# Output-projection weights of a hybrid diffusion layer: the gate's half row kept on chip while w_out is scaled, and its two parts in one raw tile

## The chip, the cores and the metric

The kernel runs on one core of one Trainium2 chip. The metric is the device time of one execution in microseconds (us). An execution with a profile also has a span, from its first to its last instruction on the engines, which is a little shorter than its time.

Five engines run side by side: PE (TensorE, matmuls, with PEld for its weight loads), DVE (VectorE), ACT (ScalarE), POOL (GpSimd) and SP (SyncE, which here issues nearly all transfers, in order). Each takes its instructions in order. Instructions of different engines wait for each other through semaphores.

## What is computed

One layer of a backbone for 2048 latent tokens of width 1024 behind a context of 256 tokens. Cut to what matters here:

```python
sh1, sc1, g1, sh2, sc2, g2 = split(ada, 6)        # ada = silu(c) @ w_ada + b_ada, rows of 1024
h = modulate(rmsnorm(x, norm_mix), sh1, sc1)
p = h @ w_in                                      # 1024 -> 3584 columns
o = concat(hgrn2_both_directions(p), spatial_gating(p))   # 4 heads of 128 each
x = x + g1 * (o @ w_out)                          # w_out is 1024 x 1024
h2 = modulate(rmsnorm(x, norm_ffn), sh2, sc2)
a, g = split(h2 @ w_up, 2)                        # 2 x 2816 columns
x = x + g2 * ((a * gelu(conv3x3(g))) @ w_down)    # w_down is 2816 x 1024
return rmsnorm(x, norm_final)
```

All inputs and the output are float32. The gates `g1` and `g2` scale columns, so `g1 * (o @ w_out)` equals `o @ (w_out * g1)`: the kernel scales the columns of the two weight matrices once, ahead of their use.

## The kernel before, in words

The large products run as three matmuls on values split in two parts: a high part, which is the value rounded to the format that PE multiplies fast (called fp32r in the profile), and a low part, the difference. `split` makes them with a cast on ACT (L133) and a difference on DVE or POOL (L134); `mm3` and `run_banks` do high x high, high x low, low x high.

**Phase one** (to about 975 us) makes `o` from `x`. It goes over the 2048 tokens in two halves of 1024. For each half and each of the four heads of the scan (`hg`), and for the four heads of the positional gating (`sgu`), it takes 128 columns of `w_in` at a time, splits them and multiplies: `run_banks` steps through a list of banks, each of 512 tokens by 128 columns in PSUM and 24 matmuls. Two banks in a row share a column block. The raw columns come into a tile `raw` (`raw_tile`, 128 x 1024 float32, a ring of three), are fetched at L221, cast to `whi` (L133) and subtracted to `wlo` (L134), one column block ahead of PE.

Between groups of three matmuls `run_banks` calls `slot()`, which lets two queues of smaller work step forward, `hg_q` and `bg_q`. Each piece of such work is a generator. When it says `yield w`, it takes its next step at the first slot after another `w` us of PE time have been issued, by the kernel's own count (`Tensor.t`). The scan's levels lie in `hg_q`: L514 (queries), L591 to L594 (keys), L794 to L801 (the diagonal), L846 (into the scores). In `bg_q` lie, from the first head on and one after the other: eight blocks of adaLN rows (`ada_block`), which leave `g1` and `g2` as rows in DRAM (`g_d`, stored at L971), then `w_out_ops`, `conv_taps` and `w_down_ops`. What `bg_q` still holds near the end of phase one is run down at once by `open_wo`.

So a generator fixes the order in which the program asks for its instructions. The build tool then puts the instructions of every engine in order by its own estimate of durations, with the program's order as priority and buffers handed out as they come free. It may take a load ahead of where the program asks for it; instructions passed through `pin` keep the program's order.

**`w_out_ops`** (L982 to L997) scales `w_out` and splits it, in 16 tiles of 128 rows by 512 columns: row blocks `k` outside, column halves `n` inside. One raw tile holds the weights in its left half and the gate's half row, spread over all 128 partitions, in its right half; both are fetched for each tile (L989, L990). After 5 us of PE time DVE multiplies (L993), ACT casts the high part into the tile `wo_hi` (tag `acc`, one buffer, which `ada_block` and `w_down_ops` use too), DVE writes the low part over the gate, and SP stores the two parts to `wo_d` (L995, L996). Another 2.5 us later the next tile begins. At the end of phase one and the beginning of the next, `wo_d` is fetched again as weights of the output projection (L916, L1145).

**`w_down_ops`** (L999 to L1011) scales `w_down` by `g2` in 22 tiles of 256 rows by 512 columns. It fetches the gate's half row once for each column half, into `acc` (L1004), then the weights (L1007), multiplies 9 us of PE time later (L1009, pinned), and stores (L1010).

**Phase two** is the output projection, the gated MLP by a scheme with seven products instead of eight, and the last norm. The change doesn't touch it.

Of the kernel before, what the change touches and what calls it, by code (L numbers as in the profile page):

```python
# [9 lines left out]
F32 = mybir.dt.float32  # L10
F32R = mybir.dt.float32r
# [7 lines left out]
P = 128  # L19
D = 1024  # L20
NK = D // P
# [27 lines left out]
def view(t, off, dims):  # L49

    return bass.AP(t.tensor, t.offset + off, [list(t.ap[0])] + [list(d) for d in dims])
# [32 lines left out]
def tile_trunk(ctx, tc, x, c, cx, c_ctx, w_ada, b_ada, norm_mix, norm_ffn, w_in, hg_norm, sgu_g, sgu_b,  # L84
               w_sp, b_sp, w_out, w_up, conv_w, conv_b, w_down, norm_final, masks, out):
    nc = tc.nc
    V, S, G, T = nc.vector, nc.scalar, nc.gpsimd, Tensor(nc.tensor)
    ld = nc.sync.dma_start
    st = nc.sync.dma_start
# [25 lines left out]
    g_d = dr.tile([2, D], F32, name="g_d")  # L115
# [3 lines left out]
    wo_d = dr.tile([P, NK, 2, D], F32, name="wo_d")  # L119
# [11 lines left out]
    def split(hi, lo, raw, eng=None, keep=lambda i: i):  # L131

        keep(S.copy(hi, raw))  # L133
        (eng or G).tensor_sub(lo, raw, hi.bitcast(F32))  # L134
# [56 lines left out]
    with es1:  # L191
        ps = es1.enter_context(tc.tile_pool(name="ps1", bufs=1, space=PSUM, reuse_waits="tile"))
        p1 = es1.enter_context(tc.tile_pool(name="p1", bufs=1, reuse_waits="tile"))
        pm = es1.enter_context(tc.tile_pool(name="pm", bufs=1, reuse_waits="tile"))
# [19 lines left out]
        def raw_tile():  # L214
            return p1.tile([P, D], F32, tag="raw", name="raw", bufs=3)
# [52 lines left out]
        acc = ph.tile([P, 2, 512], F32, tag="qs", name="acc")  # L268
# [712 lines left out]

        def w_out_ops():  # L982

            for k in range(NK):
                for n in range(2):
                    cl = slice(n * 512, n * 512 + 512)
                    raw = raw_tile()
                    w, g = raw[:, :512], raw[:, 512:]
                    ld(w, w_out[k * P:(k + 1) * P, cl])  # L989
                    ld(g, g_d[0:1, cl].broadcast_to([P, 512]))  # L990
                    yield 5.0
                    hi = pm.tile([P, 512], F32, tag="acc", name="wo_hi")
                    V.tensor_mul(w, w, g)  # L993
                    split(hi.bitcast(F32R), g.bitcast(F32R), w, V)
                    st(wo_d[:, k, 0, cl], hi)  # L995
                    st(wo_d[:, k, 1, cl], g)  # L996
                    yield 2.5  # L997

        def w_down_ops():  # L999

            for n in range(2):
                cl = slice(n * 512, n * 512 + 512)
                g = pm.tile([P, 512], F32, tag="acc", name="g2")
                ld(g, g_d[1:2, cl].broadcast_to([P, 512]))  # L1004
                for j in range(NF // 2):
                    raw = raw_tile().rearrange("p (a c) -> p a c", a=2)
                    ld(raw, w_down[2 * j * P:2 * (j + 1) * P, cl].rearrange("(a p) c -> p a c", p=P))  # L1007
                    yield 9.0
                    pin(V.tensor_mul(raw, raw, view(g, 0, [[0, 2], [1, 512]])))  # L1009
                    st(wd_d[j][:, :, cl], raw)  # L1010
                    yield 2.5  # L1011

        def silu(dst, scale):
            def f(n0, n, pj):
# [5 lines left out]
        def head(hh, h):  # L1020
# [18 lines left out]
            def pre_g():  # L1039
                if prev[0] >= 0:  # L1040
                    need(hg_q, (prev[0], prev[1], "keys"))
                else:
                    need(bg_q, "x1")
                    for e in range(8):
                        bg_q.add(ada_block(e))
                    bg_q.add(w_out_ops())
                    bg_q.add(conv_taps())
                    bg_q.add(w_down_ops())
                t["F"] = pk.tile([P, 2, TH], F32, tag="F", name="F", align_bytes=AL)
                t["K"] = pk.tile([P, 2, TH], F32, tag="K", name="K", bufs=2, align_bytes=AL)  # L1050
# [135 lines left out]
    def zbank():  # L1186
        return ps2.tile([P, 512], F32, tag="uz", name="uz", bufs=2)
# [379 lines left out]
    for n, (u, i) in enumerate(prods):  # L1567
# [10 lines left out]
        p = zbank() if i == 1 else u.z if i in (4, 6) else u.x  # L1578
        hi, lo = u.A[i]
# [40 lines left out]
    V = Kept(nc.vector, pin)  # L1620
# [243 lines left out]
```

## Time and profile before

| What | Value |
|---|---|
| median of 3 runs | 2441.4 us |
| lowest and highest of the 3 runs | 2441.0 and 2443.07 us |
| the profiled execution | 2443.78 us |
| its span | 2442.0 us |
| instructions | 32331 |
| moved by DMA in the span | 400.10 MB |
| first to last product of `w_out_ops` (L993) | 366.9 to 498.2 us |
| first to last product of `w_down_ops` (L1009) | 542.3 to 829.8 us |

How to read the rows: times are us from the span's start, unless marked ns. A group's row gives line, engine, operation and tiles (`out<-in`), then how often it ran and the durations in ns (least, median, greatest) with its first and last start. A row of waits reads "who, at which line, `<-` for whom: us in total, times, longest". A row of the timeline begins with start and duration; in brackets stands how long the engine was idle just before, and what it waited for. A row of transfers gives the size of one and the median us from its issue to its landing. A busy PE isn't PE at its peak: matmuls are pipelined and their ends are modelled, so the record of one lasts longer than its share of PE's time.

### The profile page before, as it was taken

How to read it: one execution, taken by the hardware profiler on the slowest of the kernel's cores; microseconds unless marked ns; L12 is line 12 of the kernel's file. 1: busy time of each engine (PE TensorE's matmuls, PEld its weight loads, DVE VectorE, ACT ScalarE, POOL GpSimd, SP SyncE). 2: the span in 40 equal slices, each digit the busy share in tenths (PEclk: the TensorE clock that was granted, in tenths of full speed). 3: DMA queues.
4: the chain of work that ended last, by engine and by line, in shares of the span. 5: the costliest groups of instructions: out<-in, count | busy, mean ns of one | idle time of the engine just before them, and what ended most of it. 6: DMA issues, size and time to landing. Idle time of an engine off the chain costs nothing.

```text
span 2442.0 us, 32331 instructions
## 1 busy us (share of the span) xinstructions
PE 2403.1 (98%) x11711; PEld 1994.7 (82%) x11711; DVE 1659.9 (68%) x2253; ACT 1044.4 (43%) x1802; POOL 869.2 (36%) x788
## 2 busy tenths in 40 slices
PE   8999999999999999999999999999999999999998
PEld 5887888888888887787888888888888887888887
DVE  5757796666786785465596666639866672776875
ACT  4554344444344443354544443435445442332343
POOL 0021110110122122000688788887888870000002
PEclk9999999999999999999999999999999999999999
DMA  8365446563354324668922322563222238934745
GB/s 308 120 202 165 147 147 212 186 226 124 108 175 154 105 103 162 221 208 254 312 77 89 100 77 94 175 233 101 86 94 84 86 112 338 322 122 147 228 153 197
DMA packets 307853, 400.10 MB, mean 164 GB/s; under 512 B 33113, under 2 KB 216161, under 8 KB 304621
## 3 DMA queue, kind: packets, MB, share of 16 engines
q1 hardware_dynamic: 304404, 397.28, 48.2%
q8 instruction: 92, 1.51, 0.2%
q10 hardware_dynamic: 3289, 0.76, 0.1%
q14 instruction: 68, 0.56, 0.1%
HBM read 288.85 MB, written 109.13 MB: 163 GB/s over the span
## 4 chain that ended last, share of the span: by engine, by line
PE 48%; issue 2%; DVE 1%; POOL 1%; ACT 1%; DMA 1%; SPq 0%; POOLq 0%; ACTq 0%; DVEq 0%
PE ux L65 19%; PE dn L65 15%; PE uz L65 14%; POOL ra L1723 0%; POOL rr L1724 0%; DMA raw<-in_w_up_dram 0%; DMA yf<-yd 0%; DVE dn L1434 0%; POOL Al L134 0%; ACT mhl L133 0%; ACT jk L1715 0%; DVE odd L80 0%; DVE fl L134 0%; ACT odd L1793 0%; DVE cv L1358 0%
## 5 line engine op out<-in xcount | busy, mean ns | idle before, releaser
L1434 DVE SCALAR_TENSOR_TENSOR dn<-gp,taps,dn 128x1024 f32<-128x1024 f32 x352 | 448.2, 1285 | 97.7 <-ACT dn L1431 93.3
L65 PE MATMUL dn<-thl,mhl 128*128 128x512 f32 x1680 | 381.5, 389 | 1.2 <-ACT thl L133 1.2
L65 PEld LDWEIGHTS dn<-thl,mhl 128*128 128x128 f32 x1680 | 315.0, 188 | 67.7 <-ACT thl L133 2.1
L134 POOL TENSOR_TENSOR Al<-raw,Ah 128x512 fp32r<-128x512 f32 x264 | 343.2, 1316 | 69.1 <-ACT Ah L133 42.7
L65 PE MATMUL pj<-xh,whi 128*128 128x512 f32 x896 | 362.5, 405 | 0.3 <-ACT whi L133 0.3
L65 PE MATMUL pj<-xl,whi 128*128 128x512 f32 x896 | 351.5, 392 | 0.0
L65 PE MATMUL pj<-xh,wlo 128*128 128x512 f32 x896 | 350.8, 392 | 0.8 <-DVE wlo L134 0.8
L133 ACT CAST Ah<-raw 128x512 fp32r<-128x512 f32 x264 | 162.9, 620 | 237.5 <-PE ux L65 127.7
L65 PE MATMUL ux<-xah,Ah 128*128 128x512 f32 x528 | 205.7, 390 | 0.3 <-ACT keep L1498 0.3
L65 PEld LDWEIGHTS pj<-xh,wlo 128*128 128x128 f32 x896 | 168.3, 188 | 36.8 <-DVE wlo L134 1.2
L65 PEld LDWEIGHTS pj<-xh,whi 128*128 128x128 f32 x896 | 168.7, 188 | 34.3 <-issue 3.5
L65 PEld LDWEIGHTS pj<-xl,whi 128*128 128x128 f32 x896 | 168.9, 188 | 29.9 <-DVE xl L253 0.2
L65 PE MATMUL dn<-wo,o 128*128 128x512 f32 x768 | 184.5, 397 | 2.6 <-ACT o L133 1.1
L65 PE MATMUL uz<-yf,Ah 128*128 128x512 f32 x704 | 174.0, 389 | 0.0
L65 PEld LDWEIGHTS dn<-wo,o 128*128 128x128 f32 x768 | 143.1, 189 | 32.8 <-ACT o L133 1.5
L591 POOL TENSOR_TENSOR K<-K,tot 128x512 f32<-128x512 f32 x40 | 61.1, 1526 | 300.3 <-DVE tot L521 203.9
L65 PE MATMUL ux<-yf,Ah 128*128 128x512 f32 x528 | 155.4, 389 | 0.0
L65 PEld LDWEIGHTS uz<-yf,Ah 128*128 128x128 f32 x704 | 132.1, 188 | 27.4
L65 PE MATMUL ux<-xah,Al 128*128 128x512 f32 x528 | 141.8, 390 | 1.0 <-POOL Al L134 1.0
L65 PE MATMUL ux<-xal,Ah 128*128 128x512 f32 x352 | 137.1, 389 | 0.0
L1723 POOL TENSOR_SCALAR ra<-ss 128x1 f32<-128x1 f32 x8 | 5.3, 663 | 360.4 <-ACT jk L1715 360.4
L134 DVE TENSOR_TENSOR wlo<-raw,whi 128x1024 fp32r<-128x1024 f32 x68 | 84.6, 1244 | 70.9 <-ACT whi L133 69.4
(341 smaller groups left out, 4456.1 us busy)
## 6 DMA issues: line engine op xcount, KB each, us to landing
raw<-in_w_up_dram SPq DMA_DIRECT2D x88, 512.0 KB, 3.6
mr<-m SPq DMA_DIRECT2D x85, 512.0 KB, 5.2
raw<-in_w_in_dram SPq DMA_DIRECT2D x68, 512.0 KB, 4.3
sT<-wd SPq DMA_DIRECT2D x88, 256.0 KB, 4.0
raw<-in_w_ada_dram SPq DMA_DIRECT2D x32, 512.0 KB, 4.2
yf<-yd SPq DMA_DIRECT2D x14, 1024.0 KB
m<-cv SPq DMA_DIRECT2D x22, 544.0 KB
raw<-in_w_down_dram SPq DMA_DIRECT2D x22, 512.0 KB, 3.8
```

What stands on the lines that cost most here:

```text
L65: return self.engine.matmul(out, lhsT, rhs, **kw)
L133: keep(S.copy(hi, raw))
L134: (eng or G).tensor_sub(lo, raw, hi.bitcast(F32))
L591: e.tensor_mul(view(K2, row * W + o, src), view(K, o, src), view(tot, t0, [[4, n], [ts, 2], [0, B]]))
L1434: V.scalar_tensor_tensor(out=cr, in0=gt[:, t // 3:t // 3 + RH, t % 3:t % 3 + GW], scalar=taps[:, t * NF + f:t * NF + f + 1], in1=cr, op0=A ...
L1723: G.tensor_scalar(out=a, in0=ss, scalar1=plus, scalar2=None, op0=ALU.add)
```

## The change

In `w_out_ops` the column halves become the outer loop. The gate's half row is fetched once for each half, into a tile of the tag `acc`, and stays there for eight row blocks. A raw tile now has the weights in its second half and receives the high part in its first; the low part is written over the weights. One store takes both parts to `wo_d`. The product is asked for 8 instead of 5 us of PE time after the load, and the next tile 1.5 instead of 2.5 us after the store. In `w_down_ops` the two waits go from 9 and 2.5 us to 8 and 2.

```diff
         def w_out_ops():
 
-            for k in range(NK):
-                for n in range(2):
-                    cl = slice(n * 512, n * 512 + 512)
-                    raw = raw_tile()
-                    w, g = raw[:, :512], raw[:, 512:]
+            for n in range(2):
+                cl = slice(n * 512, n * 512 + 512)
+                g = pm.tile([P, 512], F32, tag="acc", name="g1")
+                ld(g, g_d[0:1, cl].broadcast_to([P, 512]))
+                for k in range(NK):
+                    raw = raw_tile().rearrange("p (a c) -> p a c", a=2)
+                    hi, w = raw[:, 0, :], raw[:, 1, :]
                     ld(w, w_out[k * P:(k + 1) * P, cl])
-                    ld(g, g_d[0:1, cl].broadcast_to([P, 512]))
-                    yield 5.0
-                    hi = pm.tile([P, 512], F32, tag="acc", name="wo_hi")
+                    yield 8.0
                     V.tensor_mul(w, w, g)
-                    split(hi.bitcast(F32R), g.bitcast(F32R), w, V)
-                    st(wo_d[:, k, 0, cl], hi)
-                    st(wo_d[:, k, 1, cl], g)
-                    yield 2.5
+                    split(hi.bitcast(F32R), w.bitcast(F32R), w, V)
+                    st(wo_d[:, k, :, cl], raw)
+                    yield 1.5
 
         def w_down_ops():
...
-                    yield 9.0
+                    yield 8.0
                     pin(V.tensor_mul(raw, raw, view(g, 0, [[0, 2], [1, 512]])))
                     st(wd_d[j][:, :, cl], raw)
-                    yield 2.5
+                    yield 2.0
```

## The prediction

> **What bounds the kernel now.** I read the page's busy line first, then the sums by stage, then who waited for whom in the one stage that the change lives in.
>
> ```profile
> span 2442.0 us, 32331 instructions
> ## 1 busy us (share of the span) xinstructions
> PE 2403.1 (98%) x11711; PEld 1994.7 (82%) x11711; DVE 1659.9 (68%) x2253; ACT 1044.4 (43%) x1802; POOL 869.2 (36%) x788
> ```
>
> PE is the bound: 2403.1 of 2442.0 us, so 38.9 us of the whole span are idle on it. The change takes no matmul away, so it can give back only idle time of PE, and take more of it. How much of that lies where `w_out` is gated is in the sums by stage (start:end and length, then busy time with its count for PE, PE's weight loads, DVE, ACT and POOL, the granted clock of PE, the DMA share and GB/s).
>
> ```profile
> 200.00:360.00 160.00, 157.85 (x848) 132.05 (x848) 130.14 (x191) 62.56 (x103) 21.36 (x21) 1.00 0.48 149
> 360.00:515.00 155.00, 151.30 (x808) 127.20 (x807) 94.19 (x143) 68.14 (x112) 18.88 (x13) 1.00 0.63 213
> 515.00:700.00 185.00, 183.38 (x1025) 157.77 (x1025) 131.51 (x190) 78.60 (x154) 22.66 (x22) 1.00 0.43 143
> ```
>
> The stage 360 to 515 us is that of `w_out`. PE idles 155 - 151.30 = 3.70 us there, against 2.15 us before it and 1.62 us behind it, at a full granted clock (1.00). DVE is the less loaded there, 94.19 of 155 us, so it isn't short of time. It waits, and PE with it:
>
> ```profile
> PE mi L69 <- DVE nt L709: 1.3, 1, 1.3
> PE sc L65 <- ACT sig L1016: 0.8, 1, 0.8
> PE sc L65 <- DVE kl L800: 0.8, 1, 0.8
> PE mi L65 <- DVE nt L717: 0.3, 1, 0.3
> PE sc L65 <- DVE Q L514: 0.3, 1, 0.3
> PE mi L69 <- ACT vv L600: 0.2, 1, 0.2
> ```
>
> These six waits of PE (us in total, times, longest) make up the 3.70 us. Next, what DVE waited for in that stage because of `w_out`:
>
> ```profile
> DVE raw L993 <- DMA raw<-g_d: 21.3, 7, 6.5
> DVE raw L993 <- issue: 5.7, 1, 5.7
> DVE raw L993 <- DMA raw<-in_w_out_dram: 2.8, 2, 1.5
> ```
>
> DVE stands 21.3 us, in 7 waits, at the product of L993 for the gate's half row, which is fetched anew with each of the 16 tiles. Does that reach PE? Two places of the timeline say that some of it does:
>
> ```profile
> 404.98 0.69 DVE L993 TENSOR_TENSOR raw<-raw 128x512 f32<-128x512 f32 x1 [3.34 <-DMA raw<-g_d]
> ...
> 411.26 0.49 PE L65 MATMUL sc<-kh,ones_r 128*128 128x512 f32 x1
> ...
> 412.52 0.50 PE L65 MATMUL sc<-kl,ones_r 128*128 128x512 f32 x1 [0.77 <-DVE kl L800]
> ```
>
> ```profile
> 449.00 0.62 ACT L133 CAST wo_hi<-raw 128x512 fp32r<-128x512 f32 x1 [6.15 <-DVE raw L993]
> ...
> 452.25 1.02 PE L65 MATMUL sc<-Q,K 128*128 128x128 f32 x7 [0.77 <-ACT sig L1016]
> ```
>
> In the first, DVE lost 3.34 us to the gate's fetch; the three operations of the scan that it had queued behind it (L794, L795, L800) came late, and PE stood 0.77 us for the last of them. In the second, ACT's cast came 6.15 us late because it waits for that same product, the sigmoid behind it did too, and PE stood 0.77 us again. The idle time understates such a wait, because a busy matmul is longer than its share of PE's time. A stretch without waits, from the chain that ended last, has the true pace:
>
> ```profile
> 1260.04 2.72 PE ux L65 x12
> ```
>
> That is 2.72/12 = 0.23 us from one 512-column matmul to the next. The two at 411.26 and 412.52 start 1.26 us apart, so PE lost 1.03 us there where the row shows 0.77: **0.26 us more per wait**. I carry that over to the other waits as an estimate.
>
> **The change, part by part.** Rows for the prices:
>
> ```profile
> L1009 DVE TENSOR_TENSOR raw<-raw,g x22: 1208/1217/2308, 542.3 to 829.8; 128x1024 f32<-128x1024 f32 x22
> L1010 SPq DMA_DIRECT2D wd<-raw x22: 524/525/629, 543.6 to 831.0; - x22
> L989 SPq DMA_DIRECT2D raw<-in_w_out_dram x16: 328/333/839, 359.2 to 493.3; - x16
> L990 SPq DMA_DIRECT2D raw<-g_d x16: 422/424/714, 359.6 to 493.7; - x16
> ```
>
> ```profile
> raw<-in_w_in_dram SPq DMA_DIRECT2D x68, 512.0 KB, 4.3
> ...
> wd<-raw SPq DMA_DIRECT2D x22, 512.0 KB, 3.4
> ...
> raw<-in_w_out_dram SPq DMA_DIRECT2D x16, 256.0 KB, 3.6
> ...
> wo_d<-raw SPq DMA_DIRECT2D x16, 256.0 KB, 2.2
> ```
>
> 1. *Engine work.* Product, cast and difference stay, 16 times each, of the same shape; only the places of their operands move. Zero.
>
> 2. *The gate's fetch.* 16 loads become 2: 14 x 256 KB = 3.7 MB of the stage's 155 us x 213 GB/s = 33 MB go. A product then waits for one transfer (3.6 us to landing), asked 8 instead of 5 us of PE time ahead. So the 21.3 us of DVE's waits go but for two, and what ACT waits behind them. On PE the two waits traced above go, 0.77 + 0.77 = 1.54 us, and 2 x 0.26 = 0.52 us of hidden loss: **-2.1 us**. The other four (1.3 + 0.3 + 0.3 + 0.2 = 2.1 us, with 4 x 0.26 = 1.0 us hidden) end at the norm of the positional gating, at the scan and at ACT; no `w_out` instruction is named in their rows, so they lie between nothing and -3.1 us, and I book nothing.
>
> 3. *SP.* The gate's fetch, 0.42 us of issue, goes 14 times (5.9 us of SP's queue), and one store of the shape of `wd<-raw`, 0.52 us, stands for two. SP matters only through late loads: zero on the path.
>
> 4. *One raw tile and one store.* The high part leaves the single buffer `acc`. The price: a raw tile comes free when a 512 KB store lands, 3.4 us, instead of a 256 KB one, 2.2 us, and it is held from 8 instead of 5 us ahead. Raw tiles are a ring of three that the columns of `w_in` share. So some 4 us more of hold per tile; but fewer tiles at a time, since what is asked per tile rises from 7.5 to 9.5 us. `w_in`'s lead hides it, weighed as a rival below. Zero here. On the hold the Trainium skill speaks mildly against one store: its page DMA: Bandwidth & Descriptors, section Anatomy of one DMA, fits a transfer (on GpSimd's path) as about 2.0 us plus bytes over 436 GB/s, by an estimate from that page 3.2 us for 512 KB against 2.6 us for 256 KB, so 0.6 us more hold. The rows here have 1.2 us more, and the rows are used; by the page's figure the third rival would only be less likely.
>
> 5. *The gate in `acc`.* The first fetch must wait until the last `ada_block` has been summed by PE from `acc`, and the second until the eighth product. Queued behind those waits on SP are the loads of `w_in`. Both fetches have 8 us until their first product against 3.6 us to landing of a load of that size. Zero; bounded by two waits of DVE like the longest above, of which PE felt 0.77 + 0.26 = 1.0 us each: at most +2.1.
>
> 6. *`w_down` asked 8 + 2 instead of 9 + 2.5 us.* The pinned product (1.22 us) meets its load one us earlier; 8 us still cover the 4.3 us to landing of a 512 KB load. The 22 tiles took (829.8 - 542.3)/21 = 13.7 us each for 11.5 asked. The 16 tiles of `w_out` are asked 2 us more each, so `w_down` starts 32 us later, and its 22 tiles 1.5 us less, 33 us in all: it ends near the same 830 us, so the loads of gated weights at the end of phase one keep their cover. Zero, bounds -1 and +1 us.
>
> Sum -2.1 us. The profiled execution took 2443.78 us, 1.78 us around a span of 2442.0; it would become 2441.7. The median of the runs is 2441.4, 2.4 us below the profiled one; the same difference makes **2439.3 us**.
>
> **The rivals.**
>
> *Nothing is won (2441.4).* Instructions are put in order by the planner's own estimate, and loads are already hoisted as soon as a raw tile is free. If the raw ring and not the yield sets when `w_out`'s load goes out, the product still waits, now for the weights alone (2.8 us in the rows above), or the scan's products meet another queue. For it: the 5.7 us at L993 that no transfer ended. Against: 21.3 us name the gate's fetch, which goes. PE's time moves by under 1 us.
>
> *All of the stage's waits go (2436.1).* DVE and ACT are free earlier, so the norm's chain also comes in time: 3.70 us + 6 x 0.26 = 5.3 us less. Against it: the stages around still idle 2.15 and 1.62 us without any `w_out`, so some waits remain whatever is done.
>
> *The raw ring becomes the bound (2448.3).* It is slower than before. One raw tile held 4 us longer delays a load of `w_in`, whose split feeds PE's next bank.
>
> ```profile
> SPq L221 <- DMA wd<-raw: 31.4, 10, 4.8
> ```
>
> ```profile
> 609.83 0.37 SPq L221 DMA_DIRECT2D raw<-in_w_in_dram  x1
> ...
> 616.42 1.04 ACT L133 CAST whi<-raw 128x1024 fp32r<-128x1024 f32 x1 [2.58 <-PE pj L65]
> ```
>
> For it: loads of `w_in` (L221) already wait for `w_down`'s stores, 31.4 us in ten waits. Against: at the tightest place that I found behind 515 us the load leads its cast by 6.6 us, and the cast waits for PE, not for the load. It decides from the point where the delay eats that lead: 6.6 us less 4.3 us to landing leaves 2.3 us. Past it, a late column costs PE up to its cast, 1.04 us, and its difference, of the size of L1009, 1.22 us: 2.3 us. Four such columns make +9.0 us, 2441.4 - 2.1 + 9.0 = 2448.3.
>
> **How the numbers follow.** Forecast (-0.5 to -4.5 us, 2436.9 to 2440.9) 0.52; nothing won 0.18; all waits gone, or more, 0.14; the ring 0.16. A measurement of this kernel can tell about 0.2%, 4.9 us, from no change: below 2436.5 is faster, above 2446.3 slower. The all-waits case is faster but for its near end (0.03), and the forecast's far end with parts 5 and 6 on its side adds 0.04: 0.15. The ring is slower: 0.16 but for its mild end, 0.01, so 0.15. The rest, 0.70, is within. The range runs from 2434.8, past the case at 2436.1 by the 1 us of part 6 and a little more, to 2447.0, which takes in +2.1 and +1 of parts 5 and 6 and the ring's milder part; outside are some 0.04 below and 0.12 above.
>
> **What the next profile would show.** Right: the waits of L993's product for the gate's fetch gone or two, those of ACT's cast behind it mostly gone, DVE's busy time alike, PE idle in the `w_out` stage near 2 us per 155, no PE wait for `whi` or `wlo`. Ring: waits of PE for `whi` or `wlo`, longer SP waits of L221 for `wo_d` and `wd` stores. Nothing won: other waits of PE of the same sum at L514, L591, L800. I would be wrong at once if the planner's new order cost PE time in stages without `w_out`, as in the sum over 700 to 980 us; no row of the old profile can tell that.

## The result, and the profile after

The changed kernel took 2438.25 us (median of 21 runs, 2434.91 to 2441.39) against 2442.02 us before (21 runs, 2438.95 to 2444.74). The ratio is 0.9986, with a 95% interval of 0.9980 to 0.9993: 3.4 us less, between 1.7 and 4.9 (the medians themselves differ by 3.8 us). Forecast were 2439.3 us, and 2.1 us less. That is a small gain, below the 0.2% that I had set as the mark, but its interval doesn't reach 1.

Where in the program is it? In both traces the instructions of PE, DVE, ACT, POOL and SP stand in the same order up to about 350 us and from about 865 us on, so the change acts between these points. Three matmuls mark the stretch, the 289th, the 470th and the 833rd of the group `pj<-xh,whi`; up to the 470th PE's order is still the same, and by then all tiles of `w_out` are done before the change, and all but the last two after it. These are their rows of the timeline, of the kernel before and then of the changed one:

```profile
357.17 0.39 PE L65 MATMUL pj<-xh,whi 128*128 128x512 f32 x1
...
527.70 0.39 PE L65 MATMUL pj<-xh,whi 128*128 128x512 f32 x1
...
895.35 0.39 PE L65 MATMUL pj<-xh,whi 128*128 128x512 f32 x1
```

```profile
358.39 0.39 PE L65 MATMUL pj<-xh,whi 128*128 128x512 f32 x1
...
527.13 0.39 PE L65 MATMUL pj<-xh,whi 128*128 128x512 f32 x1
...
894.21 0.39 PE L65 MATMUL pj<-xh,whi 128*128 128x512 f32 x1
```

538.18 us became 535.82: the stretch is 2.4 us shorter, 1.8 us of it up to the 470th (170.53 us became 168.74), where `w_out` is scaled. The changed trace came into it 1.2 us late and gained another 2.3 us behind it. I count neither: the order there is the same, the mean granted clock of the first 60 us was 0.91 against 0.94, and behind the stretch every other trace below, with old data paths too, is shorter than the one of the kernel before. The sums by stage of the changed kernel (columns as in the prediction) have less idle time of PE in the stage of `w_out` and more in the one behind it:

```profile
200.00:360.00 160.00, 157.81 (x846) 131.81 (x845) 129.66 (x192) 62.45 (x102) 22.36 (x22) 1.00 0.49 148
360.00:515.00 155.00, 151.99 (x821) 129.04 (x820) 93.58 (x141) 66.64 (x111) 18.44 (x13) 1.00 0.54 183
515.00:700.00 185.00, 182.73 (x1021) 156.88 (x1020) 131.61 (x192) 79.28 (x156) 24.09 (x22) 1.00 0.45 146
```

PE idles 3.01 us from 360 to 515 us where it idled 3.70, and 2.27 us from 515 to 700 us where it idled 1.62. DVE and ACT are about as busy as before, and less is moved (183 against 213 GB/s). PE's waits in that stage are three instead of six:

```profile
PE sc L65 <- DVE kl L800: 2.0, 1, 2.0
PE mi L69 <- DVE nt L709: 0.6, 1, 0.6
PE pj L65 <- DVE wlo L134: 0.4, 1, 0.4
```

Three waits fewer, at the prediction's 0.26 us of hidden loss each, and 0.7 us less of idle time come to 1.5 of the 1.8 us.

So far that looks like the forecast. But here is what DVE waited for at the product of `w_out`, from its waits of the changed kernel between 360 and 515 us:

```profile
DVE raw L993 <- DMA raw<-in_w_out_dram: 28.6, 8, 7.4
...
DVE raw L993 <- DMA g<-g_d: 6.0, 1, 6.0
```

Before, it was 21.3 + 5.7 + 2.8 = 29.8 us, most of it for the gate. Now it is 34.6 us, most of it for the weights. DVE's waits didn't go; they passed from one transfer to another. SP's own waits from 360 to 540 us in the changed kernel show what the load of the weights stands behind:

```profile
SPq L995 <- DVE raw L134: 52.5, 14, 6.0
SPq L991 <- DMA wo_d<-raw: 21.2, 9, 4.0
```

L991 is the load of the next tile's weights. Nine times SP holds it until the store of the tile before (L995) has landed, since only then is a raw tile free; and that store has waited on SP, in front of the load, for DVE's difference. One such round, from SP's timeline and from DVE's:

```profile
396.65 0.37 SPq L995 DMA_DIRECT2D wo_d<-raw  x1
401.08 0.33 SPq L991 DMA_DIRECT2D raw<-in_w_out_dram  x1
```

```profile
395.94 0.69 DVE L134 TENSOR_TENSOR raw<-raw 128x512 fp32r<-128x512 f32 x1 [0.73 <-ACT raw L133]
404.00 0.69 DVE L993 TENSOR_TENSOR raw<-raw,g 128x512 f32<-128x512 f32 x1 [7.38 <-DMA raw<-in_w_out_dram]
```

Difference, store, landing, load, landing, product: most tiles of `w_out` run one after the other through one raw tile. At nine of the eleven loads from 390 to 495 us the other two raw tiles hold columns of `w_in` that were fetched ahead. So the product follows its load by 5.3 us in the mean of the 16 tiles, as it did before (5.4 us), whatever the 8 us in the program say.

The rows of transfers of the changed kernel that answer to those of before:

```profile
wo_d<-raw SPq DMA_DIRECT2D x16, 512.0 KB, 2.8
...
raw<-in_w_out_dram SPq DMA_DIRECT2D x16, 256.0 KB, 3.4
```

The single store lands after 2.8 us. I had taken 3.4 us from the like-sized `wd<-raw`; the estimate from the Trainium skill (DMA: Bandwidth & Descriptors, Anatomy of one DMA), for GpSimd's path, was 3.2 us, nearer but also above. In e10, below, the same store took 3.2 us.

### The profile page after: what moved, and what is told of

It is laid out like the page before. It is cut to its first block, busy times and chain, and to the rows that moved or that the text cites. A ratio compares the mean times of both kernels' runs of the same rounds, so it can differ in the third digit from the quotient of the medians.

```text
span 2438.6 us, 32286 instructions
## 1 busy us (share of the span) xinstructions
PE 2402.0 (99%) x11711; PEld 1995.0 (82%) x11711; DVE 1656.9 (68%) x2253; ACT 1043.2 (43%) x1802; POOL 867.8 (36%) x788
## 4 chain that ended last, share of the span: by engine, by line
PE 54%; issue 2%; DMA 1%; DVE 1%; POOL 1%; ACT 1%; SPq 0%; POOLq 0%; ACTq 0%; DVEq 0%
PE dn L65 20%; PE ux L65 19%; PE uz L65 14%; PE pj L65 0%; POOL ra L1722 0%; DMA raw<-in_x_dram 0%; POOL rr L1723 0%; PE ux L69 0%; DMA raw<-in_w_up_dram 0%; DMA yf<-yd 0%; PE uz L69 0%; DVE dn L1433 0%; DMA yd<-fl 0%; POOL Al L134 0%; DVE cv L1357 0%
```

## The experiments

Theories, as the expectations name them. **Gate**: the fetch of the gate's half row for each tile cost PE its waits, and keeping it on chip wins them back. **Ring** or **tile**: the product waits for a raw tile to come free, as shown above. **Order**: each edit makes the planner put the instructions into another order, and what is won or lost is where DVE's waits fall among the scan's instructions. **Asks**: the waits in the `yield`s matter by themselves.

The table has for each kernel the ratio to the kernel before (11 runs each, but 21 for the changed one and 4 for e9) with its 95% interval, and from its one trace the idle time of PE from 360 to 540 us and DVE's wait at the product of `w_out`. In e9 the stage lies some 15 us later.

| kernel | ratio (interval) | PE idle, us | DVE's wait, us |
|---|---|---|---|
| before | 1 | 3.82 | 29.8 |
| changed | 0.9986 (0.9980 to 0.9993) | 3.12 | 34.6 |
| a0, changed again | 0.9989 (0.9980 to 0.9998) | 2.81 | 33.6 |
| e7, changed and two small POOL operations | 0.9985 (0.9976 to 0.9994) | 1.50 | 31.8 |
| e1, w_out's part alone | 0.9998 (0.9989 to 1.0007) | 3.84 | 35.9 |
| e2, w_down's asks alone | 1.0002 (0.9993 to 1.0011) | 5.18 | 31.6 |
| e3, new data paths, old asks | 0.9992 (0.9983 to 1.0001) | 1.80 | 28.8 |
| e4, old data paths, new w_out asks | 1.0017 (1.0009 to 1.0026) | 7.17 | 37.2 |
| e5, gate fetched per tile | 0.9998 (0.9989 to 1.0006) | 4.47 | 30.5 |
| e6, two stores | 0.9999 (0.9990 to 1.0008) | 3.72 | 31.8 |
| e10, new data paths, old w_out asks, new w_down asks | 0.9983 (0.9974 to 0.9992) | 1.70 | 29.3 |
| e8, no engine work on w_out | 0.9979 (0.9971 to 0.9988) | 0.69 | none |
| e12, no load of w_out | 0.9982 (0.9974 to 0.9991) | 1.12 | 10.2 |
| e9, loads of w_in pinned | 1.0103 (1.0090 to 1.0117) | - | 36.4 |

The idle time leaves one cost out, the clock. In the traces of e1, e4 and e6, and in no other between 360 and 540 us, the granted clock of PE fell to half for 3.4 us soon after PE's longest wait. First e1's wait, then its sums (columns as before) right behind it:

```profile
415.94 0.50 PE L65 MATMUL sc<-kl,ones_r 128*128 128x512 f32 x1 [2.07 <-DVE kl L800]
```

```profile
417.40:420.60 3.20, 3.20 (x9) 2.43 (x9) 3.17 (x5) 1.52 (x3) 0.00 (x0) 0.50 0.43 164
```

PE is busy all the time there, but its matmuls start 0.43 us apart instead of 0.23: by my estimate 1.7 us lost on top of the wait. It came behind waits of 2.07 us (e1), 3.6 us (e4) and 3.06 us (e6), and not behind others of 1.77 us (a0), 1.99 us (changed) and 2.47 us (e4).

**a0_after_again**, the changed kernel with no edit:

> The changed kernel once more, with a second trace, to see how far one trace's stage sums repeat: time 2 to 5 us below before; DVE's waits at the w_out product (L993) again 30 to 38 us by both theories that are left; the stretch that holds w_out within 2 us of the first trace.

It repeats: 2439.85 us against 2442.06. Its second trace has the same waits as the first (33.6 us of DVE, one wait of PE for `kl` of 1.8 us).

**e8_no_work** and **e12_no_load** bound what can be won. e8 has no product, cast, difference or raw tile for `w_out`:

```diff
-                    V.tensor_mul(w, w, g)
-                    split(hi.bitcast(F32R), w.bitcast(F32R), w, V)
-                    st(wo_d[:, k, :, cl], raw)
+                    for h in range(2):
+                        ld(wo_d[:, k, h, cl], w_out[k * P:(k + 1) * P, cl])
```

> Leaves out the scaling by g1 and the split: w_out is copied twice from DRAM to DRAM in the same rhythm, so DVE, ACT and the raw ring see nothing of w_out. The floor of what any form of this step can win. Theory gate or ring (w_out's waits reach PE): PE idle in the w_out stage falls to near 1.5 us, time 3 to 6 us below before. Theory order (stalls come from the scan's own chains): PE idle stays at 2.5 to 4 us there, time within 2 us of the changed kernel.

e12 keeps all engine work and the store, and takes only the load away, so that the product waits for no weights:

```diff
-                    ld(w, w_out[k * P:(k + 1) * P, cl])
-                    V.tensor_mul(w, w, g)
+                    V.tensor_mul(w, g, g)
```

> Leaves out the load of the weights in w_out_ops: DVE multiplies the gate by itself, all else (product, cast, difference, store, asks) as in the changed kernel. Theory tile: DVE's waits at the product vanish, PE idle in the w_out stage falls to that of the copy without work (0.6 us for 360 to 515 us), time 1 to 3 us below the changed kernel. If it is the engine work of w_out, not its waits, that delays the scan: PE idle stays at 1.5 to 3 us there.

In e8 a single wait of PE is left from 360 to 515 us:

```profile
PE mi L69 <- DVE nt L709: 0.5, 1, 0.5
```

The sums by stage of e8, then of e12:

```profile
360.00:515.00 155.00, 154.42 (x835) 131.75 (x835) 78.67 (x115) 61.24 (x100) 15.63 (x13) 1.00 0.37 124
```

```profile
360.00:515.00 155.00, 154.30 (x827) 131.08 (x827) 95.15 (x139) 67.16 (x112) 18.98 (x13) 1.00 0.49 171
```

With 95.15 us of DVE's work instead of 78.67, e12 leaves PE as free as e8 does: 0.70 us of idle against 0.58. The engine work of `w_out` costs PE next to nothing; the load, with the products that wait for it, costs it the rest. (e12 takes away the transfer and its hold of a raw tile along with the wait; the timelines show the wait.) That is the step of the prediction on which the gain rests, and it holds. The whole prize is 0.21% of 2442 us, 5.1 us (2.9 to 7.1); the change took about two thirds of it in its median.

**e1_out_only** and **e2_down_only** split the change in two:

```diff
 # e1: the changed kernel, but in w_down_ops
-                    yield 8.0
+                    yield 9.0
...
-                    yield 2.0
+                    yield 2.5
 # e2: the kernel before with the opposite edit
```

> The change in w_out_ops alone; w_down_ops asks 9 and 2.5 us as before. Theory gate (the fetch of the gate's half row cost PE its waits): all of the gain, 3 to 4 us below before. Theory order (waits of DVE stay, and what is gained or lost is where they fall among the scan's instructions): the w_out stage as in the changed kernel, about 1.8 us gained up to 515 us, the stages of w_down as before, so 1 to 3 us below before in all.

> Only the two waits of w_down_ops changed, to 8 and 2 us. Theory gate: nothing, within 0.5 us of before. Theory order: another order behind 540 us, so stalls of PE there move by 1 to 2 us either way, while the w_out stage keeps its 3.7 us of idle PE.

Neither part shows a gain by itself; together they do. By the order of instructions e1 is the changed kernel up to about 573 us, and e2 the kernel before up to about 557 us. Yet PE idles 3.84 us in e1's `w_out` stage against 3.12 and 2.81, and 5.18 in e2's against 3.82. And e7, below, has the order of the changed kernel there on PE, DVE, ACT and SP, with 1.50 us. So four traces of one order have 1.5 to 3.8 us of idle PE, presumably because the products wait for transfers whose landing varies: smaller differences in the table's third column say nothing. The interval of e1 (-2.7 to +1.7 us) overlaps that of the changed kernel (-4.9 to -1.7); how the gain divides between the two parts is open.

**e3_old_asks**, **e4_asks_only** and **e10_old_out_new_down** separate data paths from asks:

```diff
 # e3: the changed kernel with w_out asked 5.0 and 2.5, w_down 9.0 and 2.5
 # e10: the changed kernel with w_out asked 5.0 and 2.5
-                    yield 8.0
+                    yield 5.0
                     V.tensor_mul(w, w, g)
                     split(hi.bitcast(F32R), w.bitcast(F32R), w, V)
                     st(wo_d[:, k, :, cl], raw)
-                    yield 1.5
+                    yield 2.5
 # e4: the kernel before with w_out asked 8.0 and 1.5
```

> The changed data paths (gate on chip, parts in one raw tile, one store), but asked as before: 5 and 2.5 us, w_down 9 and 2.5. Theory gate: nearly all of the gain stays, 2 to 4 us below before, and DVE's waits at the w_out product fall well below 29.8 us. Theory order: DVE still waits 25 to 40 us there, and the time lies between 2 us below and 2 us above before.

> The old data paths (gate fetched for each tile, two stores), asked as in the changed kernel: 8 and 1.5 us for w_out, w_down as before. Theory gate: no gain, DVE's waits for the gate stay near 21 us or grow. If the longer ask hides the fetch by itself: DVE's waits there fall below 10 us and 2 us are gained without the gate on chip. Theory order: waits stay, time within 2 us of before either way.

> The changed data paths with w_out asked as before, 5 and 2.5 us, and w_down asked as changed, 8 and 2 us. Theory asks (the longer ask of w_out costs, the shorter one of w_down gains a little): the best of all, 3 to 6 us below before. If the longer ask of w_out is needed: at or above the changed kernel's time.

The longer ask in the old data paths makes the kernel slower by 4.2 us (2.2 to 6.3), the one clear loss besides e9. As I read it, the product is put later in DVE's order, but its load can't go out earlier. DVE then waits longer (37.2 us against 29.8), and PE behind it; these are PE's waits in e4 from 360 to 540 us:

```profile
PE mi L69 <- DVE nt L709: 3.6, 1, 3.6
PE sc L65 <- DVE kl L800: 2.5, 1, 2.5
PE sc L65 <- DVE Q L514: 1.0, 1, 1.0
```

The 3.6 us are the wait behind which the clock fell. The new data paths with the old ask are 2 us below before (-4.2 to +0.2), with DVE's wait still at 28.8 us, and with `w_down`'s new ask e10 is the fastest form that does the whole work: 2436.9 against 2441.51 us, 0.9983. It beats the kernel before; its interval overlaps that of the changed kernel, so it isn't shown to beat that one too. Its sum in the `w_out` stage:

```profile
360.00:515.00 155.00, 153.36 (x826) 130.25 (x825) 96.44 (x145) 68.61 (x113) 17.63 (x13) 1.00 0.57 193
```

1.64 us idle, against 3.01 in the changed kernel, but 1.38 in e7 with the changed kernel's order.

Read as pairs that differ in the data paths alone, these runs say where the gain is from. With `w_out` asked as changed and `w_down` as before, e1 (0.9998) stands against e4 (1.0017); with `w_out` asked as before and `w_down` as changed, e10 (0.9983) against e2 (1.0002); with both asked as before, e3 (0.9992) against the kernel before. The new data paths are faster each time, by some 2 to 4.6 us, and in the first two pairs the intervals don't overlap, though the gaps between them are small. So the gain is from the data paths, and "asked for further ahead" isn't where it is from.

**e5_refetch** and **e6_two_stores** take back one data path each:

```diff
 # e5: inside the loop over k, after the load of the weights (the same two lines ahead of the loop go)
+                    g = pm.tile([P, 512], F32, tag="acc", name="g1")
+                    ld(g, g_d[0:1, cl].broadcast_to([P, 512]))
 # e6
-                    st(wo_d[:, k, :, cl], raw)
+                    st(wo_d[:, k, 0, cl], hi)
+                    st(wo_d[:, k, 1, cl], w)
```

> The changed kernel, but the gate's half row is fetched anew for each of the 16 tiles, into the buffer acc, as before into the raw tile. Theory gate (having it on chip pays): 2 to 4 us slower than the changed kernel, back near before. Theory tile (a product waits for the weights, whose load waits for a raw tile; the gate has its own buffer and lands meanwhile): within 1 us of the changed kernel, DVE's waits at the product 30 to 40 us as there.

> The changed kernel with two 256 KB stores for each tile instead of one of 512 KB. Theory tile: a raw tile comes free about 1.2 us earlier (2.2 against 3.4 us to landing), the next load goes out earlier, and DVE's waits at the product fall by some 5 to 10 us; time 0 to 1 us better. If the one store pays through SP's queue: 1 us or more slower.

Both land at the time of the kernel before (0.9998 and 0.9999), against my expectation from the tile theory in both cases. The changed kernel wasn't run beside them, and both intervals overlap with its three (0.9986, 0.9989 and 0.9985), so that either data path gains by itself isn't shown. For the gate the medians agree with the old price of 2 us. For the store I had expected a little less time. What e6's trace loses against the changed one in the `w_out` stage lies in one place of its timeline:

```profile
400.16 0.69 DVE L993 TENSOR_TENSOR raw<-raw,g 128x512 f32<-128x512 f32 x1 [5.94 <-DMA raw<-in_w_out_dram]
...
408.21 0.69 DVE L993 TENSOR_TENSOR raw<-raw,g 128x512 f32<-128x512 f32 x1 [3.32 <-DMA raw<-in_w_out_dram]
...
414.47 0.73 PE L65 MATMUL sc<-kh,ones_r 128*128 128x512 f32 x2 [3.06 <-ACT kh L798]
```

Two products that wait 5.94 and 3.32 us stand in DVE's order ahead of the scan's diagonal, and PE stands 3.06 us for it, with the fall of the clock behind that. The sum of DVE's waits is lower than in the changed kernel (31.8 against 34.6 us); it is their place that costs. Whether two stores would cost as much in another order isn't settled.

**e7_ring2** was to take one of the three raw tiles away during `w_out`:

```diff
+            hold = raw_tile()
+            G.memset(hold[:, :8], 0.0)
             for n in range(2):
...
+            G.tensor_copy(hold[:, 8:16], hold[:, :8])
```

> The changed kernel with one of the three raw tiles taken away while w_out is scaled (held by a few bytes that POOL writes and reads). Theory ring (a raw tile's way from store to free to next load sets when w_out's product can run): DVE's waits at L993 grow or w_in's columns come late, PE idles 5 to 20 us more in the w_out stage. If the ring doesn't matter: within 1 us of the changed kernel.

It tested nothing of the kind. The planner put the closing copy right behind the memset (POOL's timeline of e7), since nothing made it wait:

```profile
359.90 0.10 POOL L985 MEMSET raw<- 128x8 f32 x1 [4.68 <-DVE acc L961]
360.06 0.96 POOL L999 COPY raw<-raw 128x8 f32<-128x8 f32 x1
```

The tile was free again after a microsecond. On PE, DVE, ACT and SP e7 has the order of the changed kernel, and POOL has the two small operations more: it is in effect the changed kernel, and a third sample of its gain.

**e9_pin_w_in** was to free raw tiles by keeping `w_in`'s loads back:

```diff
-            ld(raw, w_in[...])
+            (pin if key[1] == 512 else lambda i: i)(ld(raw, w_in[...]))
```

> The changed kernel with w_in's column loads kept in the program's order, so that they are not taken far ahead and hold no raw tile for 10 to 30 us. Theory ring: the loads of w_out go out earlier and DVE's waits at L993 fall from some 35 to below 12 us; PE gains up to 2 us if no w_in column comes late, and loses 1 to 2 us per late column otherwise. If the ring isn't what holds w_out's loads: the waits stay above 25 us.

25 us slower, and DVE's waits at the product stay at 36.4 us. PE's two longest waits from 350 to 880 us:

```profile
PE pj L65 <- ACT whi L133: 5.6, 4, 2.6
PE sc L65 <- ACT kh L798: 1.4, 1, 1.4
```

PE now waits for `whi`, and it did so before the `w_out` stage as well (3.6 us of the 14.2 us of idle from 60 to 360 us, against 4.2 us of idle in all in the changed kernel). Around three waits of 2.3 to 3.3 us there, the last of them for `whi`, PE ran some 13.6 us at half clock besides. The pin moved far more than the loads beside `w_out`, so it says nothing against the serial chain that SP's waits show; it does show what the loads of `w_in` taken far ahead are worth. A ring of four raw tiles, the direct test, wasn't run.

## Why the prediction was right, and where it wasn't

**The bound and the place: right.** PE is the bound, the change could only act on its idle time in phase one, and the stretch between 357 and 895 us holds 2.4 us of gain in the traces. Idle PE in the `w_out` stage, for which I had named near 2 us, came to 3.0 us there.

**That product waits reach PE: shown** by e8 and e12. The two places traced for it went different ways. The wait for the sigmoid (0.77 us) is gone. The wait for `kl` grew from 0.77 to 2.0 us, by the same mechanism with the weights in the gate's place: DVE waits 7.38 us at the product at 404.00 us, in front of the diagonal, and again at the next one, right in front of `kl`:

```profile
413.77 0.69 DVE L993 TENSOR_TENSOR raw<-raw,g 128x512 f32<-128x512 f32 x1 [1.74 <-DMA raw<-in_w_out_dram]
414.38 1.22 DVE L800 TENSOR_TENSOR kl<-Q,kh 128x1024 fp32r<-128x1024 f32 x1
```

**The step that failed** is the middle of part 2: "So the 21.3 us of DVE's waits go but for two." They passed to the load of the weights, 28.6 us in 8 waits, and ACT's waits for the product behind them stayed too (13.9 us before, 15.3 us now, from 360 to 515 us). The first rival had named the reason, that the raw ring and not the `yield` sets when the load goes out, but with the result that nothing is won. In truth DVE's wait stayed and PE's loss still shrank. The price of -2.1 us measured -3.4 (-1.7 to -4.9) for the change as a whole; that it came out near was in good part luck, since the two waits that it priced, 1.54 us together, are one of 2.0 us in the changed trace. The gain is from the data paths, as the pairs show, and e5 agrees with the gate as one contribution; how it reaches PE is open. The waits that I booked at nothing moved: the norm of the positional gating went from 1.3 to 0.6 us, and `nt` at L717, `Q` and `vv` (0.3, 0.3 and 0.2 us) are gone. An order by which fewer waits fall in front of what PE needs next is my reading of that; for e6 it is shown in the timeline, for the change as a whole only argued.

**Asked 8 us ahead: wrong** as a part of the gain. The distance from load to product is 5.3 us against 5.4, and e4 shows the longer ask as a cost where the data paths are old.

**One store at nothing: open.** The hold that I feared was somewhat smaller (2.8 us to landing in the changed trace, not 3.4), and e6 without the merged store lost the gain in its median, with an interval that overlaps that of the changed kernel.

**The gate in `acc`: as bounded.** Its first fetch held DVE once for 6.0 us (the row with `g<-g_d` above), and no wait of PE names it.

**`w_down`'s asks: bounds of 1 us perhaps too narrow.** From e3 to e10 the medians differ by 2.1 us and from e1 to the changed kernel by 2.9 us, both for the better, while e2 shows nothing; all these intervals overlap. The schedule came out earlier than I had worked out: the first product of `w_down` at 569.2 us instead of some 574 us, and the last at 816.8 us instead of near 830.

**The ring as the bound on PE: did not come.** PE waited 0.4 us once for `wlo`. That late columns of `w_in` cost PE time is real, though: e9 is 25 us slower, with PE waiting for `whi`; but it is the pin that makes them late there, not the ring.

## What to carry to other kernels

When a wait for one transfer is taken away, ask which transfer of the same step lands next, and what its issue is queued behind: here the load stood on SP behind a store that stood behind DVE, and a longer ask in the program couldn't move it. To price such background work, run it once without its loads and once without its work; that told what was to be won at all (5 us) and that it hung on the load. Where a planner orders the instructions, judge an edit of a few us by many runs, and by pairs of variants that differ in one thing: one order had 1.5 to 3.8 us of idle PE in one stage in four traces, so a single trace can't rank orders that lie closer. And look at the granted clock behind each long wait of PE.

## What the runs showed of the hardware

Work on DVE and ACT beside a full PE was almost free: 16.5 us more of DVE's work and 5.9 us more of ACT's in one stage (e12 against e8, one trace each) left PE 0.12 us more idle, while two products that waited 5.94 and 3.32 us in DVE's queue left PE idle for 3.06 us (e6).

A wait of PE could cost again through the clock: in three traces of the `w_out` stage one of 2.07 to 3.6 us was soon followed by 3.4 us at half the granted clock, some 1.7 us of PE's time by my estimate; the three waits of 1.77 to 2.47 us named above were not.

And the same program on the same chip spreads over some 6 us (2434.91 to 2441.39 us in 21 runs), more than the whole gain, so that only medians over many runs can tell it. The clock goes along with this: of the 33 runs of the kernel before that e10 is compared with, those with a mean granted clock of 0.996 have a median of 2444.8 us, those with 0.997 2442.1 us, with 0.998 2440.4 us and with 0.999 2438.6 us. In the first 60 us, ahead of anything that the edits touch, the mean granted clock was 0.94 in the trace of the kernel before, 0.91 in that of the changed one and 1.00 in e12's.
